# A fifth raw-weight buffer and a softmax denominator summed in one operation

## The chip, the core and the metric

The kernel runs on one core of a Trainium2 chip. The metric is the device time of one execution in microseconds; of several executions the median counts. Inside a core, TensorE (PE) multiplies matrices and has a separate row in the profile for loading weights (PEld); VectorE (DVE), ScalarE (ACT) and GpSimd (POOL) work on tiles; SyncE (SP) issues most of the DMA transfers. Each engine works through its own queue in order, and an instruction that waits holds up all that stands behind it on that engine.

## The reference, cut to what matters

Two layers of a diffusion backbone. 512 latent tokens and 256 context tokens, model width 1024. Each layer has one input projection into three groups of heads (short convolution, windowed attention with a sink, gated linear attention, below called GLA), one output projection, and a SwiGLU block of width 2816. The part that the change touches is the attention's softmax:

```python
def softmax_with_sink(scores, sink):
    s = broadcast(sink, scores.shape[:-1] + (1,))
    p = softmax(concatenate([s, scores], axis=-1), axis=-1)
    return p[..., 1:]

def one_block(qi, i):                       # 128 queries; 8 heads, 2 key heads
    s_ctx = q @ k_ctx                       # 256 context keys
    s_loc = where(valid, q @ ks, -inf)      # up to 3 blocks of 128 keys
    p = softmax_with_sink(concatenate([s_ctx, s_loc]) * HEAD_DIM ** -0.5, sink)
    return p[..., :L] @ v_ctx + p[..., L:] @ vs
```

The sink is one learned number per head that enters the denominator and has no value of its own. Layer 0 also computes attention for the 256 context tokens (over the context keys alone); layer 1 does not.

## The kernel before, in words

Activations stand transposed, features on the 128 partitions, tokens along the free axis. Nearly every float32 product is taken as three products of rounded parts: a value is split into a high part (`whi`, rounded to fp32r) by ScalarE and a low part (`wlo`, the difference) by VectorE, and TensorE runs high times high, high times low, low times high.

**Weights.** A list (`plan`) holds all weight pieces in the order of their use, up to 512 KB each, and among them the pieces of `w_mod`, from which the modulation vectors are made. `w_load` (DMA issue at L523) walks the list and issues the loads on SP's queue. The destinations are the tiles `raw`, a ring of `RAWS = 4` buffers: a load is emitted only once the piece four places earlier has been read, and on the chip it waits until that buffer's readers are done. `w_advance` splits the next piece into `whi` and `wlo` (two buffers each). A `w_mod` piece is not split: either TensorE reads it from `raw` (32-column products with `cst`), or VectorE sums it row by row (`t<-raw,cst,t`, L199).

**Order.** A planner (`Plan`) writes the program out. It keeps an estimated clock for each engine, adds the cost of each operation, and lets short chains of work (`attn_task`, `gla_task`, the pieces of the modulation) in between the large products when their operands should be ready and buffers are free. `ROOM` tells it how many buffers each pool has: `main` and `bank` are banks of PSUM, `act` large tiles, `t3` the temporaries that the profile calls `t`. Until the first products of layer 0 are done (`S.strict`), each engine's order is pinned to the planner's; after that it follows the planner where nothing else decides.

**One attention task** (`attn_task`, 40 of them: 24 in layer 0, of which 8 on context queries, and 16 in layer 1; 32 have local keys) takes one head of each of the two key heads and 128 queries. TensorE makes scores, VectorE takes their maximum (`mx`) and from it `nm`, the negative of the scaled maximum, bounded by the sink. ScalarE takes the exponentials with `nm` as bias and sums each row on the side (`accum_out` into `den` and `den2`; in the profile each such sum is an ACTIVATION_READ_ACCUMULATOR). Then `es` becomes the reciprocal of the denominator: VectorE adds `psink` and `nm`, ScalarE takes the exponential, VectorE adds `den`, adds `den2` where there are local keys, and inverts. TensorE transposes the probabilities, multiplies them with the values, and with `es` broadcast (`bank<-tab,es`) turns the denominators into rows.

**Silu of the gate.** The tiles `gg0` and `gg1` of the input projection go through Silu on ScalarE as they leave TensorE. Silu and Exp are in different tables of ScalarE. `preload` and the Silu itself bring the table loads (ACT_TABLE_LOAD).

The tile `zero` (128 by 512, bfloat16) is the moving operand of 22 products that warm TensorE or open and close shared PSUM banks.

Of the kernel before, what the change touches and what calls it, by code (L numbers as in the profile page):

```python
# [11 lines left out]
BF16 = mybir.dt.bfloat16  # L12
U8 = mybir.dt.uint8
AF = mybir.ActivationFunctionType
ALU = mybir.AluOpType
AX = mybir.AxisListType

P = 128
# [17 lines left out]

LAG = 2600
LAG_F = 2100
ROOM = dict(main=3, bank=5, act=20, t3=14)


XS = (0, SX, 0)
# [48 lines left out]
class Plan:  # L91
# [141 lines left out]
    def free(self, owner=None):  # L233

        now = self.clk["pe"]
        self.live = [e for e in self.live if e[2] is None or e[2] > now]
        left = dict(ROOM)
        used = {g: dict.fromkeys(ROOM, 0) for g in self.kept}
        for e in self.live:
# [80 lines left out]
def hybrid_kernel(ctx: ExitStack, tc: tile.TileContext, x, c, cx, c_ctx, w_mod, b_mod, norm1_g, norm2_g,  # L320
                  w_in, conv_w, attn_sink, gla_gate_w, gla_gate_b, gla_norm_g, w_out, w_up, w_down,
                  final_norm_g, table, out):
    nc = tc.nc
    S = Plan(tc)
    const = ctx.enter_context(tc.tile_pool(name="const", bufs=1))
    wp = ctx.enter_context(tc.tile_pool(name="wp", bufs=2))
    act = ctx.enter_context(tc.tile_pool(name="act", bufs=ROOM["act"]))
    t3 = ctx.enter_context(tc.tile_pool(name="t3", bufs=ROOM["t3"]))
    small = ctx.enter_context(tc.tile_pool(name="small", bufs=4))
    dram = ctx.enter_context(tc.tile_pool(name="dram", bufs=1, space=bass.MemoryType.DRAM))  # L330

    psum = {k: ctx.enter_context(tc.tile_pool(name=k, bufs=ROOM[k], space=bass.MemoryType.PSUM))
            for k in ("main", "bank")}

    def bank(kind="bank"):
        return S.took(kind, psum[kind].tile([P, 512], F32, tag=kind, name=kind))
# [7 lines left out]
    def sm(n, name, bufs=None):  # L344
        return small.tile([P, n], F32, tag=name, name=name, bufs=bufs)


    RAWS = 4
    plan = []

    def cols(src, n):
# [158 lines left out]
    def w_load():  # L510
        while at["dma"] < len(plan):
# [4 lines left out]
            else:  # L516
                if len(ring) >= RAWS and not ring[-RAWS]["read"]:
                    break
                ring.append(it)
                raw = wp.tile([P, 1024], F32, tag="raw", name="raw", bufs=RAWS)  # L520
            it["raw"] = raw[:, :it["n"] * it["width"]].rearrange("p (k n) -> p k n", k=it["n"])
# [107 lines left out]
    psink = const.tile([P, 16], F32, name="psink")  # L629
# [1 line left out]

    ones = const.tile([P, 1], F32, name="ones")
    nc.gpsimd.memset(ones, 1.0)
    zero = const.tile([P, 512], BF16, name="zero")
    nc.gpsimd.memset(zero, 0.0)
    epsc = const.tile([P, 1], F32, name="epsc")
    nc.gpsimd.memset(epsc, EPS)

# [133 lines left out]
    class Opened:  # L772
# [20 lines left out]
        def close(self, evict):  # L793
            for s, pt in zip(self.segs, self.pts):
                self.chunks([len(self.X) - 1], s, pt)
                evict(self.w[0], s, pt)
                S.gave(pt)
            S.poll()

    class Firsts:  # L800
# [5 lines left out]
        def open(self):  # L806
            n = len(self.widths)
            whole = self.pair[0][1] - self.pair[0][0] == 512
            m = ROOM["main"] if whole else 1
            S.room(main=m, bank=n - m + (2 if whole else 0))  # L810
            px = [bank("main" if i < m else "bank") for i in range(n)]
            pc = [bank() for _ in range(n // 2)] if whole else []
            a, b = self.pair
            self.banks = px, pc
            self.at = {a: [(px[i], 0) for i in range(n)],
                       b: [(pc[i // 2], i % 2 * 256) if whole else (px[i], 256) for i in range(n)]}

            self.shared = pc if whole else px
            for pt in self.shared:
                S.mm(pt, zero[:, :P], zero, True, False)  # L820

        def weights(self, q):
            self.parts[q] = w_next((*self.key, q))
# [15 lines left out]

        def close(self):  # L840
            for pt in self.shared:
                S.mm(pt, zero[:, :P], zero, False, True)
            S.poll()

        def run(self, norm, evict, hook=None):
# [635 lines left out]
    def attn_task(l, b, g, st):  # L1481

        loc = [t for t in (b - 1, b, b + 1) if 0 <= t < 4] if b < 4 else []
# [27 lines left out]
        sk = slice(l * 8 + g, l * 8 + g + 5, 4)  # L1511
        nm = sm(2, "nm")
        S.stt(nm, mx, -0.125, nsink[:, sk], ALU.mult, ALU.min)
        den = sm(2, "den")
        den2 = sm(2, "den2")
        st["todo"][g] -= 1
        if st["todo"][g] == 0:
            S.gave(Q)
# [3 lines left out]
        pr = [tmp(), tmp()]  # L1522
        for kv in range(2):
            S.act(pr[kv][:, :256], pc[:, kv * 256:(kv + 1) * 256], AF.Exp, bias=nm[:, kv:kv + 1], scale=0.125,
                  accum_out=den[:, kv:kv + 1])
            if loc:
                S.act(pr[kv][:, 256:nkeys], pl[kv][:, :nl], AF.Exp, bias=nm[:, kv:kv + 1], scale=0.125,
                      accum_out=den2[:, kv:kv + 1])
        S.gave(pc, *pl)
        es = sm(2, "es")  # L1530
        S.tt(es, nm, psink[:, sk], ALU.add)
        S.act(es, es, AF.Exp)
        S.tt(es, es, den, ALU.add)
        if loc:
            S.tt(es, es, den2, ALU.add)
        S.recip(es, es)

        n = len(tiles)
# [2 lines left out]
        pt = [bank() for _ in range(3 if loc else 1)]  # L1541
# [92 lines left out]
    r = rstd(ssum, NT, between)  # L1634
    pt = bank()
    for _ in range(WARM):
        S.mm(pt, zero[:, :P], zero, True, True)
    S.gave(pt)
    pv = bank()
    S.tr(pv[:, :16], vrow[:16, 0, :], ident[:16, :16])  # L1640
# [7 lines left out]
    for t0, t1, _ in (XS, CS):  # L1648
        pt = bank()
# [85 lines left out]
    for l in range(DEPTH):  # L1735
# [104 lines left out]
        def after(name):  # L1840
# [21 lines left out]
            elif name == "v":  # L1862
                tasks["v"] = S.spawn(tokens_task(tmps.pop(name), st["V"]), prio=-1)
            elif name[0] == "q":
                qr = tmps.pop(name)
                rope(qr)
                S.room(act=1)
                Q = act_t(F32R)
                for kv in range(2):
                    own = slice(kv * 64, kv * 64 + 64)  # L1870
                    oth = slice(64 - kv * 64, 128 - kv * 64)
                    S.acopy(Q[own, kv, :n], qr[own, :n])
                    S.tt(Q[oth, kv, :n], qr[own, :n], Q[own, kv, :n].bitcast(F32), ALU.subtract)
                st["q"][i] = Q
                S.gave(qr)
                at_ = max(S.last, st["tk"])

                def when():
                    return max(at_, tasks["v"]["ready"]) if tasks["v"]["done"] else None
                for b in range(nblk):  # L1880
                    tasks["attn"].append(S.spawn(attn_task(l, b, i, st), prio=10 + i, group=("attn", 3), when=when))
# [151 lines left out]
        else:  # L2033
# [3 lines left out]
            def final_task(seg, sums):  # L2037
# [10 lines left out]
                for t in range(nt):  # L2048
                    yield dict(bank=2)
                    pts = [bank(), bank()]  # L2050
                    for k in range(NK):
                        S.tr(pts[k // 4][:, (k % 4) * P:(k % 4 + 1) * P], xT[k][:, t0 + t * P:t0 + (t + 1) * P], ident)
                    o = wp.tile([P, 1024], F32, tag="raw", name="raw", bufs=RAWS)
                    S.ts(o[:, :512], pts[0], r[:, t:t + 1], None, ALU.mult)
# [33 lines left out]
```

## Time and profile before

| | us |
|---|---|
| median of 3 runs | 1610.41 |
| lowest and highest | 1608.43, 1613.43 |
| the profiled execution, its own time | 1607.56 |
| its span, from the first to the last instruction | 1605.8 |
| TensorE busy in it | 1576.7 |
| VectorE busy | 1197.3 |
| ScalarE busy | 763.7 |

The granted clock of TensorE was 0.999 over the span. Busy times of TensorE include the modelled ends of overlapping products, so a gap between two products of less than about 0.17 us doesn't show as idle: a product with 512 columns has a mean duration of some 0.40 us, yet in dense stretches the next one begins 0.23 us after it. Where a row of a timeline says x5, five instructions of one kind are merged; what stands in brackets at its end is idle time ahead of it and what ended it.

### The profile page before, as it was taken

What the parts mean: (1) busy time and instruction counts of PE and PEld (TensorE: products, weight loads), DVE (VectorE), ACT (ScalarE), POOL (GpSimd) and SP (SyncE); (2) the same over time, 40 slices, a digit from 0 to 9 for tenths busy, and PEclk for the clock granted to TensorE, in tenths of its full rate; (3) what the DMA queues carried; (4) which work ended last, traced back from release to release, by engine and by line L of the source; (5) the groups of instructions that cost most, each with busy time, mean ns of one, the idle gap of its engine ahead of it and who ended that gap; (6) DMA issues with size and microseconds to landing.
All of it is one profiled execution on the core that took longest, in us unless ns stands there. A gap on an engine that the chain in (4) does not pass through costs nothing.

```text
span 1605.8 us, 29431 instructions
## 1 busy us (share of the span) xinstructions
PE 1576.7 (98%) x11684; PEld 1392.3 (87%) x11690; DVE 1197.3 (75%) x2386; ACT 763.7 (48%) x1634; POOL 105.2 (7%) x122
## 2 busy tenths in 40 slices
PE   7999999999999999999999999999999999999998
PEld 5777777888889899999999988787879999989898
DVE  5686967658895887788888877869777956757476
ACT  4454635553663243242433546455564744536254
POOL 2000000000000000000000010000001112213012
PEclk9999999999999999999999999999999999999999
DMA  9832221243224544535334342211224466858652
GB/s 267 255 100 55 77 82 37 68 157 107 78 80 131 169 136 122 167 121 153 94 107 129 91 132 66 54 28 54 67 89 116 86 153 144 174 132 159 144 122 92
DMA packets 277578, 184.39 MB, mean 115 GB/s; under 512 B 30853, under 2 KB 258753, under 8 KB 277441
## 3 DMA queue, kind: packets, MB, share of 16 engines
q1 hardware_dynamic: 251008, 155.93, 33.9%
q0 software_dynamic: 24608, 21.27, 7.7%
q10 hardware_dynamic: 1824, 5.31, 0.8%
q8 instruction: 92, 1.51, 0.4%
q14 instruction: 46, 0.37, 0.1%
HBM read 175.14 MB, written 7.34 MB: 114 GB/s over the span
## 4 chain that ended last, share of the span: by engine, by line
PE 82%; DVE 7%; ACT 2%; issue 2%; DMA 1%; DVEq 0%; ACTq 0%
PE main L139 53%; PE bank L139 26%; PE bank L143 3%; DVE act L188 3%; DVE t L188 1%; ACT t L155 1%; DMA raw<-in_w_mod_dram 1%; DVE mx L207 1%; DVE wlo L188 1%; DVE t L216 1%; DVE t L199 0%; DMA raw<-in_w_up_dram 0%; ACT whi L177 0%; ACT act L155 0%; ACT t L177 0%
## 5 line engine op out<-in xcount | busy, mean ns | idle before, releaser
L139 PE MATMUL main<-act,whi 128*128 128x512 f32 (+2 forms) x2772 | 665.4, 345 | 3.5 <-ACT act L155 1.8
L139 PEld LDWEIGHTS main<-act,whi 128*128 128x128 f32 x2772 | 460.0, 189 | 63.1 <-issue 11.6
L139 PE MATMUL main<-act,wlo 128*128 128x512 f32 (+2 forms) x1866 | 478.3, 334 | 1.2 <-DVE wlo L188 1.2
L139 PEld LDWEIGHTS main<-act,wlo 128*128 128x128 f32 x1866 | 314.8, 189 | 27.7 <-DVE wlo L188 2.7
L177 ACT CAST whi<-raw 128x512 fp32r<-128x512 f32 (+4 forms) x242 | 181.4, 751 | 286.3 <-PE main L139 198.9
L139 PE MATMUL bank<-act,whi 128*128 128x256 f32 (+2 forms) x1140 | 208.4, 309 | 0.4 <-DVE whi L188 0.4
L139 PEld LDWEIGHTS bank<-act,whi 128*128 128x128 f32 x1140 | 178.2, 190 | 7.1 <-DVE whi L188 0.8
L139 PE MATMUL bank<-act,wlo 128*128 128x256 f32 (+2 forms) x898 | 170.8, 308 | 0.1
L199 DVE SCALAR_TENSOR_TENSOR act<-main,mods,act 128x256 f32<-128x256 f32 (+1 forms) x162 | 99.0, 615 | 79.0 <-PE main L139 77.8
L188 DVE TENSOR_TENSOR wlo<-raw,whi 128x1024 fp32r<-128x1024 f32 (+4 forms) x122 | 123.1, 1009 | 33.1 <-ACT whi L177 28.9
L139 PEld LDWEIGHTS bank<-act,wlo 128*128 128x128 f32 x898 | 142.6, 190 | 3.9 <-DVE wlo L188 0.6
L177 ACT COPY t<-bank 128x512 f32<-128x512 f32 (+3 forms) x171 | 67.7, 411 | 111.7 <-PE bank L139 96.0
L188 DVE TENSOR_TENSOR wlo<-raw,wlo 128x512 fp32r<-128x512 f32 x120 | 81.7, 686 | 40.4 <-ACT wlo L177 39.8
L199 DVE SCALAR_TENSOR_TENSOR t<-raw,cst,t 128x512 f32<-128x512 f32 x126 | 92.0, 746 | 16.8 <-DMA raw<-in_w_mod_dram 16.1
L188 DVE TENSOR_TENSOR whi<-raw,whi 128x512 fp32r<-128x512 f32 x120 | 81.4, 686 | 27.4 <-ACT whi L177 25.9
L155 ACT ACTIVATE t<-bank,nm 128x256 f32<-128x256 f32 (+1 forms) x144 | 69.9, 498 | 55.8 <-DVE nm L199 52.0
L177 ACT CAST wlo<-raw 128x512 fp32r<-128x512 f32 x120 | 74.6, 622 | 41.3 <-PE main L139 18.9
L188 DVE TENSOR_TENSOR act<-t,act 128x128 fp32r<-128x128 f32 (+7 forms) x150 | 84.3, 575 | 9.5 <-ACT act L177 8.7
L177 ACT CAST act<-t 128x128 fp32r<-128x128 f32 (+6 forms) x142 | 71.6, 521 | 34.0 <-DVE t L188 28.9
L188 DVE TENSOR_TENSOR t<-bank,t 128x256 f32<-128x256 f32 (+4 forms) x129 | 55.4, 431 | 39.9 <-ACT t L177 30.5
L139 PE MATMUL main<-act 128*128 128x256 f32 (+1 forms) x516 | 78.5, 308 | 0.0
L155 ACT ACTIVATE t<-t 128x256 f32<-128x256 f32 (+3 forms) x108 | 58.0, 537 | 40.9 <-DVE t L188 40.3
(161 smaller groups left out, 2012.7 us busy)
## 6 DMA issues: line engine op xcount, KB each, us to landing
raw<-in_w_mod_dram SPq DMA_DIRECT2D x92, 512.0 KB, 4.1
raw<-in_w_up_dram SPq DMA_DIRECT2D x80, 512.0 KB, 4.7
raw<-in_w_in_dram SPq DMA_DIRECT2D x26, 512.0 KB, 3.9
t<-in_w_up_dram POOLq DMA_DIRECT2D x40, 256.0 KB, 5.3
raw<-in_w_down_dram SPq DMA_DIRECT2D x24, 384.0 KB, 4.6
raw<-in_w_down_dram SPq DMA_DIRECT2D x32, 256.0 KB, 2.9
raw<-in_w_down_dram SPq DMA_DIRECT2D x16, 320.0 KB, 3.5
raw<-in_w_up_dram POOLq DMA_DIRECT2D x20, 256.0 KB, 4.7
```

The source lines that it names most:

```text
L139: self.pin("pe", self.nc.tensor.matmul(out, lhsT, rhs, start=start, stop=stop, **kw))
L143: self.pin("pe", self.nc.tensor.transpose(out, in_, ident))
L155: ins = self.pin("act", self.nc.scalar.activation(out, in_, func, **kw))
L177: self.pin("act", self.nc.scalar.copy(out, in_))
L188: self.pin(eng, self._v(eng).tensor_tensor(out, a, b, op))
L199: self.pin(eng, self._v(eng).scalar_tensor_tensor(out, a, s, b, op0, op1))
L207: self.pin("dve", self.nc.vector.tensor_reduce(out, in_, AX.X, op))
L216: self.pin("dve", self.nc.vector.copy_predicated(out, mask, data))
```

## The change

Four edits. `RAWS` becomes 5, and `ROOM["t3"]` becomes 13 in exchange. The tile `zero` shrinks to 128 by 128 (`zeros`), and where 512 columns are needed one of its columns is read with a broadcast. In `attn_task` one tile holds all parts of the denominators in columns: for each of the two heads the sum over context keys, the sum over local keys if there are any, and the exponential of the sink. That exponential is taken by two ScalarE operations of one column each, with `nm` as bias, straight from `psink`; one reduction on VectorE sums the columns.

```diff
-ROOM = dict(main=3, bank=5, act=20, t3=14)
+ROOM = dict(main=3, bank=5, act=20, t3=13)
...
-    RAWS = 4
+    RAWS = 5
...
-    zero = const.tile([P, 512], BF16, name="zero")
-    nc.gpsimd.memset(zero, 0.0)
+    zeros = const.tile([P, P], BF16, name="zeros")
+    nc.gpsimd.memset(zeros, 0.0)
+    zero = zeros[:, :1].to_broadcast([P, 512])
...
-        den = sm(2, "den")
-        den2 = sm(2, "den2")
+
+        nd = 3 if loc else 2
+        den = sm(2 * nd, f"den{nd}")
...
             S.act(pr[kv][:, :256], pc[:, kv * 256:(kv + 1) * 256], AF.Exp, bias=nm[:, kv:kv + 1], scale=0.125,
-                  accum_out=den[:, kv:kv + 1])
+                  accum_out=den[:, kv * nd:kv * nd + 1])
             if loc:
                 S.act(pr[kv][:, 256:nkeys], pl[kv][:, :nl], AF.Exp, bias=nm[:, kv:kv + 1], scale=0.125,
-                      accum_out=den2[:, kv:kv + 1])
+                      accum_out=den[:, kv * nd + 1:kv * nd + 2])
         S.gave(pc, *pl)
         es = sm(2, "es")
-        S.tt(es, nm, psink[:, sk], ALU.add)
-        S.act(es, es, AF.Exp)
-        S.tt(es, es, den, ALU.add)
-        if loc:
-            S.tt(es, es, den2, ALU.add)
+        for kv in range(2):
+            S.act(den[:, (kv + 1) * nd - 1:(kv + 1) * nd], psink[:, l * 8 + g + 4 * kv:l * 8 + g + 4 * kv + 1], AF.Exp,
+                  bias=nm[:, kv:kv + 1])
+        S.red(es, den.rearrange("p (a b) -> p a b", a=2), ALU.add)
         S.recip(es, es)
```

Since the planner's costs, its buffers and the moment of each load change, the order of instructions changes too, in the two attention and GLA stages for the most part. Counted over the program, VectorE loses 112 small additions and gains 40 reductions, ScalarE loses 40 small exponentials and gains 80, and two table loads; TensorE, POOL and SP keep their instructions. On TensorE 818 lines of some 10,000 stand elsewhere, and the number of changes from one kind of product to another is the same before and after.

On VectorE, in the second attention task of layer 0, from its `nm` to its reciprocal (`act<-act` and `t_1085` are GLA work in between; `mx_1542` belongs to the task after it). Before:

```order
L199 SCALAR_TENSOR_TENSOR nm<-mx,nsink 128x2
L216 COPY_PREDICATED t_1085<-lvm,bank 128x384
L188 TENSOR_TENSOR es<-nm,psink 128x2
L188 TENSOR_TENSOR act<-act 128x12x2x32
L207 TENSOR_REDUCE mx<-bank 128x2
L188 TENSOR_TENSOR es<-es,den 128x2
L188 TENSOR_TENSOR act<-act 128x2x12
L207 TENSOR_REDUCE mx_1542<-bank 128x1
L188 TENSOR_TENSOR es<-es,den_1489 128x2
L207 TENSOR_REDUCE mx_1542<-bank 128x1
L220 RECIPROCAL es<-es 128x2
```

And after, at the same place:

```order
L199 SCALAR_TENSOR_TENSOR nm<-mx,nsink 128x2
L216 COPY_PREDICATED t_1087<-lvm,bank 128x384
L188 TENSOR_TENSOR act<-act 128x12x2x32
L207 TENSOR_REDUCE mx<-bank 128x2
L188 TENSOR_TENSOR act<-act 128x2x12
L207 TENSOR_REDUCE mx_1541<-bank 128x1
L207 TENSOR_REDUCE es<-den_1489 128x2
L207 TENSOR_REDUCE mx_1541<-bank 128x1
L220 RECIPROCAL es<-es 128x2
```

Three additions went, and one reduction stands between two maxima of the next task.

On ScalarE, at the Silu of `gg1` in layer 0 (`t_3845` and `t_3876` before, `t_3818` and `t_3890` after, are its latent and its context half; the other rows are attention tasks). Before:

```order
L155 ACTIVATE es<-es 128x2
L155 ACT_TABLE_LOAD
L155 ACTIVATE t_3845<-main 128x512
L155 ACTIVATE t_3876<-main 128x256
L166 ACT_TABLE_LOAD
L177 CAST act<-t_3845 128x512
L177 CAST act<-t_3876 128x256
L155 ACTIVATE t_3905,den<-bank,nm 128x256
```

And after:

```order
L155 ACTIVATE den_3802<-psink,nm 128x1 x2
L155 ACT_TABLE_LOAD
L155 ACTIVATE t_3818<-main 128x512
L166 ACT_TABLE_LOAD
L177 CAST act<-t_3818 128x512
L155 ACTIVATE t_3868,den_3867<-bank,nm 128x256 x2
L155 ACTIVATE t_3869,den_3867<-bank,nm 128x256 x2
L155 ACTIVATE den_3867<-psink,nm 128x1 x2
L177 COPY t_3803<-bank 128x256
L155 ACT_TABLE_LOAD
L155 ACTIVATE t_3890<-main 128x256
L166 ACT_TABLE_LOAD
```

The two halves were under one pair of table loads and are now under a pair each, with an attention task's exponentials between them.

On SP, near the end of the first layer's first products (`t_832` and `csn` are the constants of the masks and of the rotary embedding):

```order
 L523 DMA raw<-in_w_in_dram 128x8x64 x2
-L644 DMA t_832<-in_table_dram 128x768
-L645 DMA csn<-in_table_dram 128x1024
 L523 DMA raw<-in_w_mod_dram 128x4x256
+L645 DMA t_834<-in_table_dram 128x768
+L646 DMA csn<-in_table_dram 128x1024
 L523 DMA raw<-in_w_in_dram 128x8x128
```

One more weight load is issued ahead of the constants. It is the only place where SP's order changes.

## Rows read from the trace of the kernel before

**Rows 1.** The page, part 1: busy time, share of the span, instructions.

```profile
PE 1576.7 (98%) x11684; PEld 1392.3 (87%) x11690; DVE 1197.3 (75%) x2386; ACT 763.7 (48%) x1634; POOL 105.2 (7%) x122
```

**Rows 2.** Windows: busy us of each engine (instructions), then PEclk, DMA share, GB/s.

```profile
20.00:60.00 40.00, 36.59 (x382) 29.22 (x381) 24.14 (x54) 16.16 (x30) 0.00 (x0) 1.00 1.00 251
...
250.00:350.00 100.00, 99.75 (x834) 82.12 (x832) 65.05 (x199) 56.51 (x180) 2.14 (x4) 1.00 0.26 85
...
610.00:720.00 110.00, 109.24 (x652) 101.55 (x651) 84.32 (x143) 36.27 (x65) 0.00 (x0) 1.00 0.45 136
```

**Rows 3.** Waits of PEld, 102 to 440 us: us in total, times, longest.

```profile
PEld bank L139 <- ACT t L177: 3.7, 6, 1.1
...
PEld bank L143 <- DVE t L203: 0.8, 2, 0.7
...
PEld bank L139 <- ACT es L155: 0.4, 1, 0.4
...
PEld bank L139 <- DVE es L188: 0.2, 1, 0.2
```

**Rows 4.** The same, 1000 to 1310 us.

```profile
PEld bank L139 <- ACT t L177: 4.5, 8, 1.4
...
PEld bank L139 <- DVE act L188: 1.2, 3, 0.7
...
PEld bank L139 <- DVE t L188: 0.2, 1, 0.2
PEld bank L143 <- ACT act L177: 0.2, 1, 0.2
```

**Rows 5.** Groups by shape: busy us, mean ns of one, idle before and releasers.

```profile
L155 ACT ACTIVATE t<-bank,nm 128x256 f32<-128x256 f32 x112 | 52.2, 475 | 55.8 <-DVE nm L199 52.0 <-PE main L139 1.6 <-DVE es L220 1.3
...
L155 ACT ACTIVATE t<-bank,nm 128x384 f32<-128x384 f32 x32 | 18.6, 581 | 0.0
...
L188 DVE TENSOR_TENSOR es<-es,den 128x2 f32<-128x2 f32 x72 | 11.2, 155 | 16.1 <-ACT es L155 15.4
...
L207 DVE TENSOR_REDUCE mods<-bank 128x4 f32<-128x16 f32 x8 | 1.4, 172 | 9.3 <-PE bank L143 9.3
```

**Rows 6.** Timeline of ACT around the Silu of gg1, layer 0: start, us.

```profile
328.04 0.47 ACT L155 ACTIVATE t<-bank,nm 128x256 f32<-128x256 f32 x1 [2.51 <-DVE nm L199]
328.41 0.19 ACT L155 ACTIVATION_READ_ACCUMULATOR t<-bank,nm 128x1 f32 x1
...
330.07 0.21 ACT L155 ACTIVATE es<-es 128x2 f32<-128x2 f32 x1
330.16 0.49 ACT L155 ACTIVATE t<-bank,nm 128x256 f32<-128x256 f32 x1
...
331.30 1.28 ACT L155 ACT_TABLE_LOAD   x1
332.60 0.87 ACT L155 ACTIVATE t<-main 128x512 f32<-128x512 f32 x2
```

**Rows 7.** Waits of VectorE, whole span.

```profile
DVE t L199 <- DMA raw<-in_w_mod_dram: 16.1, 16, 4.0
```

**Rows 8.** Timelines of ACT, then PE, 34 to 37 us.

```profile
34.27 1.00 ACT L177 CAST whi<-raw 128x960 fp32r<-128x960 f32 x1 [0.67 <-DMA raw<-in_w_in_dram]
...
36.51 0.50 PE L139 MATMUL main<-act,wlo 128*128 128x512 f32 x1 [0.69 <-DVE wlo L188]
```

**Rows 9.** Timelines of DVE, then PE, 637 to 641 us.

```profile
637.91 0.75 DVE L199 SCALAR_TENSOR_TENSOR t<-raw,cst,t 128x512 f32<-128x512 f32 x1 [4.03 <-DMA raw<-in_w_mod_dram]
...
640.50 0.50 PE L139 MATMUL main<-act,wlo 128*128 128x512 f32 x1 [0.17 <-DVE wlo L188]
```

**Rows 10.** The tile csn: its readers, and its DMA.

```profile
L188 DVE TENSOR_TENSOR t<-t,csn x20: 674/689/702, 77.4 to 1098.9; 128x512 f32<-128x512 f32 x20
L645 SPq DMA_DIRECT2D csn<-in_table_dram x1: 434/434/434, 64.2 to 64.2; - x1
...
DMA to landing us min/median/max: 4.4/4.4/4.4
```

More of the change, by code (lines that the diff above doesn't have):

```diff
@@ L819, in open @@
             for pt in self.shared:
-                S.mm(pt, zero[:, :P], zero, True, False)
+                S.mm(pt, zeros, zero, True, False)
         def weights(self, q):
@@ L841, in close @@
             for pt in self.shared:
-                S.mm(pt, zero[:, :P], zero, False, True)
+                S.mm(pt, zeros, zero, False, True)
             S.poll()
@@ L1636, in hybrid_kernel @@
     for _ in range(WARM):
-        S.mm(pt, zero[:, :P], zero, True, True)
+        S.mm(pt, zeros, zero, True, True)
     S.gave(pt)
```

## The prediction

> **What bounds the kernel now.** I read the page's busy times first, then the windows by stage, then what TensorE's weight loads wait for, and last the timelines of the places where a wait shows. TensorE is busy for 1576.7 of 1605.8 us [rows 1]. What it doesn't fill is 29.1 us, and that is the most that any edit which leaves its products alone can return, apart from gaps too short to show. It is less in the stages: between 250 and 350 us, where attention tasks run among the projections, TensorE is busy 99.75 of 100 us, VectorE 65.05 and ScalarE 56.51 [rows 2]. The two slower engines there have time to spare in sum and matter only by their latency: a product waits when the tile that it needs comes out of a queue a little late.
>
> So the question for every edit is not how much busy time it takes off VectorE or puts on ScalarE, but how much of that reaches a waiting product. The waits of the weight loads tell which engine is the late one. From 102 to 440 us they wait for ScalarE in 7 rows, from 3.7 us down to 0.4 us, 8.3 us together, and for VectorE in 8 rows, from 0.8 down to 0.2 us, 3.6 us together [rows 3]. From 1000 to 1310 us it is 9 rows for ScalarE, from 4.5 down to 0.2 us, together 11.4 us, and 7 for VectorE, from 1.2 down to 0.2 us, together 4.0 us [rows 4]. ScalarE is late by 19.7 us, VectorE by 7.6 us. These are upper bounds, since a weight load can wait while the product before it still runs. The denominators themselves hardly appear: products wait for `es` in rows of 0.4 and 0.2 us [rows 3].
>
> **The sum.** I make it against the profiled execution, 1607.56 us, which is 1.76 us more than its span and 2.85 us under the median of the three runs.
>
> *The denominators on VectorE.* An addition on two columns takes 155 ns [rows 5]. The change takes out 72 additions of `den` and 40 of `psink`, 112 by 0.155, 17.4 us, and puts in 40 reductions. A reduction of 16 columns to 4 takes 172 ns [rows 5]; for 4 or 6 columns I take the same, 6.9 us. VectorE's busy time falls by 10.5 us. How much of it reaches a product lies between nothing and the 7.6 us that weight loads wait for VectorE. The two stages are some 550 us long, and at the share of the window at 250 us [rows 2] VectorE works some 360 us in them; 10.5 us are 3% of that, and 3% of 7.6 us is 0.2 us. I take -0.2. The wait in these chains does not go: VectorE stood 15.4 us, in front of the first addition, until the exponential of `es` was there [rows 5]. Now the reduction stands there and waits for ScalarE's last column.
>
> *The denominators on ScalarE.* One exponential of two columns goes, two of one column with `nm` as bias come, 40 times. The old one occupied the engine for 0.09 us, from 330.07 to the next start at 330.16 [rows 6]. For the new one the nearest row is the exponential with the same bias on 256 columns: it starts at 328.04 and the engine goes on at 328.41 [rows 6], 0.37 us. The step from 256 to 384 columns, 475 to 581 ns [rows 5], gives 0.83 ns a column, so 256 columns are 0.21 us and what remains for one column is 0.16 us. Bounds for one: 0.09 us, as the old one without a bias tile, and 0.37 us. At 0.16 a task gains 2 by 0.16 less 0.09, 0.23 us, and all 40 gain 9.2 us; at the bounds 3.6 and 26 us. Queued behind these 0.23 us on ScalarE are the copies of the transposed probabilities, evictions and the next weight's high part. The engine has idle time in every one of these stages, 43 of 100 us in the window at 250 us [rows 2], and gives most of it back there. By the same share it works some 310 us in the two stages; 9.2 us are 3% of that, and 3% of the 19.7 us is 0.6 us. I take +0.6, and keep 0 and 9.2 as ends; 26 us would need the old neighbour's 256 columns in an operation that has one, so I don't carry that end.
>
> The Trainium skill (ScalarE: Activation LUTs, What ACT_TABLE_LOAD costs) states 186 ns plus 0.833 ns a column for an activation, 93 ns more when the bias is a column of a tile, and an overlap of 93 ns between neighbours. The slope agrees with the trace; by the page a new exponential occupies 0.19 us instead of my 0.16, and the 40 tasks would add some 11 us by that estimate. No row shows one on a single column.
>
> *The chain of one task.* The last column is there later by 0.23 us less the little that the additions took: one addition of 155 ns fewer follows in the tasks with local keys, none in the 8 others. The denominators come 0.1 to 0.2 us later. Ahead of their use lie the transposes, their copies and a stretch of large products, and the waits for `es` were 0.4 and 0.2 us [rows 3]. Nothing on the path; if that cover were gone it would be at most 40 by 0.2, 8 us.
>
> *The second pair of table loads at `gg1`.* The Silu of the context half now has loads of its own. One load takes 1.28 us and the Silu begins 1.30 us after its start [rows 6], so ScalarE gets 2.6 us more at that place. What waits behind them are the copies of an attention task and the high part of the next weight, and after them the output projection, whose first pass is over the latent tokens and doesn't need the context half. ScalarE is idle nearly half of the time there. I take 0, between 0 and 2.6. The Trainium skill (same page, same section) counts 1.28 us for the load and 1.38 us more to drain, 2.66 us for each switch, and asks to group activations by table. By it the pair costs 5.3 us; the row shows that the engine goes on 0.02 us after the load, so I stay with 2.6.
>
> *The fifth raw buffer.* A load can now be issued one piece earlier. It helps where a product waits for something that waited for a load. Two such places show: at 34.27 us ScalarE waits 0.67 us for a load and 2 us later TensorE stands for 0.69 us [rows 8]; at 637.91 us VectorE has waited 4.03 us for a piece of `w_mod`, behind which stand an eviction and the low part of a weight, and at 640.50 us TensorE stands for 0.17 us [rows 9]. VectorE's waits for such loads come to 16.1 us in 16 places [rows 7]. Those are the two ends: nothing, and -16.1 us if each were on the path and went. Between 20 and 60 us the DMA engines are full, share 1.00 [rows 2]; an earlier issue lands no earlier there, it only joins the line. Between 610 and 720 us the share is 0.45 [rows 2], and an earlier issue does land earlier. Of the 16.1 us only a few tenths reach TensorE in the one place that I can follow, so I take an eighth, -2.0.
>
> *The constants behind one more load.* On SP the tables are issued behind a load that waits for its buffer. `csn` was issued at 64.2 us, landed 4.4 us later, and is first read at 77.4 us [rows 10]: over 8 us of slack. Nothing.
>
> *`zeros` and one `t3` tile fewer.* The products with `zeros` have the same shape and number; the broadcast read is not in the trace. I take 0: the 22 products have their old number of columns, and a slower read would show on them alone. One temporary fewer shows only through the order.
>
> *The order.* TensorE has the same products and as many switches from kind to kind, so no stage gets denser by design. Which waits fall where is drawn anew in the two stages: 27.3 us of waits [rows 3, 4], of which I let a fifth go either way, 5.5 us. I take 0.
>
> Sum: -0.2 +0.6 +0 +0 -2.0 +0 +0 +0 = -1.6 us, 1606.0 us for an execution like the profiled one, and 1610.41 - 1.6 = 1608.8 us on the median. That is 0.1% less. About 0.3%, 4.8 us, is what a measurement of this kernel can tell from no change, so I forecast no change.
>
> **The rivals.** *ScalarE becomes the late engine (slower).* The 0.23 us of every task falls ahead of the copies on which products wait most, 3.7 and 4.5 us in the first rows [rows 3, 4]. If all of it passes, with the pair of table loads, it is 9.2 + 2.6 = 11.8 us, 1622 us on the median; half of it, some 6 us, gives 1616. It decides from about 4.8 us on, when over 40% passes. For it: ScalarE is the later engine of the two by more than two to one. Against it: the idle time beside it.
>
> *The fifth buffer takes most of the late loads (faster).* If the places of [rows 7] held back evictions and through them the products by half, it is -8 us, 1602. For it: in-order VectorE stands up to 4 us at a time with evictions behind it. Against it: TensorE stood 0.17 us after the longest one [rows 9], because several banks were open.
>
> *The order alone.* The stages shift by 5.5 us one way or the other, 1605 or 1616. For it: 818 places on TensorE differ. Against it: the planner works by the same rules, and the kinds of waits stay.
>
> *The fifth buffer does nothing.* The splits into `whi` and `wlo` still have two buffers each, and these set the pace; then -2.0 falls away and 1610.8 us is left.
>
> **How the numbers follow.** The forecast gets 0.40; ScalarE late 0.17 (0.13 of it over 0.3%); late loads 0.18 (0.15 over 0.3%); the order 0.15 (0.07 each way); the buffer without effect 0.10. Faster by over 0.3%: 0.15 + 0.07 = 0.22. Slower: 0.13 + 0.07 = 0.20. Within: 0.58. The range reaches from the late loads at -8 us, with a little of the order's gain, to ScalarE late by half: 1600 to 1617 us.
>
> **What would show it.** In the profile of the changed kernel: VectorE's busy time lower by about 10 us and ScalarE's higher by 9 to 14 us; a small exponential that occupies ScalarE for 0.16 us; VectorE's wait in front of the reduction still near 15 us; two more table loads around the Silu of `gg1`; VectorE's waits for `w_mod` well under 16.1 us; and TensorE's idle time within 5 us of 29. I would be wrong if the weight loads' waits for ScalarE grew by over 5 us in the two stages, or if the waits for loads fell and the span fell by as much.

## The result and the profile after

The changed kernel is slower: 1619.09 us on the median of 6 runs (1617.89 to 1623.18) against 1610.34 us of the kernel before (1608.43 to 1613.43), a ratio of 1.0049 with the interval 1.0029 to 1.0069. I had forecast 1608.8 us and a range up to 1617: the sign is wrong and the time lies above the range. The profiled execution took 1617.89 us with a span of 1616.1. The one of the kernel before, 1607.56 us, is faster than each of its six runs, so the two profiles lie 10.3 us apart where the medians lie 8.8 apart.

The page's busy times, then the windows of the stretches of [rows 2] and of a short one at the first place below (length, busy us of PE, PEld, DVE, ACT, POOL with their instructions, granted clock, DMA share, GB/s):

```profile
PE 1582.0 (98%) x11684; PEld 1399.3 (87%) x11690; DVE 1194.8 (74%) x2314; ACT 775.8 (48%) x1676; POOL 104.3 (6%) x122
```

```profile
20.00:60.00 40.00, 37.31 (x378) 29.95 (x379) 23.92 (x53) 15.49 (x30) 0.00 (x0) 0.96 1.00 257
250.00:350.00 100.00, 97.95 (x795) 80.75 (x796) 60.18 (x166) 59.69 (x183) 2.14 (x4) 0.98 0.25 85
610.00:720.00 110.00, 109.32 (x656) 102.53 (x655) 87.09 (x144) 38.55 (x67) 0.00 (x0) 1.00 0.45 133
262.90:266.30 3.40, 3.40 (x18) 3.01 (x16) 2.58 (x11) 2.87 (x10) 0.00 (x0) 0.50 0.49 154
```

Against [rows 1] VectorE is busy for 2.5 us less and ScalarE for 12.1 us more. But TensorE is busy for 5.3 us more with the same 11,684 products, and its idle time grows from 29.1 to 34.1 us. The fourth window shows where the busy time comes from: for 3.4 us after 262.9 us the granted clock is 0.50, that is 1.2 instead of 2.4 GHz, and each product takes longer. Over the whole span the mean granted clock is 0.995, against 0.999 before. Not all of that is the change's: the 0.96 of the first window stands in g2_all_oldorder below too. In the attention window at 250 us TensorE does 795 products instead of 834 [rows 2].

I counted how late each product starts against the kernel before, the same product in both. The profiled execution ends 10.6 us later, and three places make up most of it: 3.2 us around 262 us, 2.8 us around 530 us, some 4 us between 1105 and 1130 us. What lies between and behind them nearly cancels; in the attention stages the figure swings by several us where products have changed places.

**The first place, layer 0's attention.** ScalarE, then TensorE, of the changed kernel (start, duration, operation, idle time and its releaser):

```profile
260.32 1.04 ACT L177 CAST whi<-raw 128x1024 fp32r<-128x1024 f32 x1 [3.50 <-PE main L139]
261.27 0.47 ACT L155 ACTIVATE t<-bank,nm 128x256 f32<-128x256 f32 x1
...
263.29 0.48 ACT L155 ACTIVATE den<-psink,nm 128x1 f32<-128x1 f32 x2
263.66 0.58 ACT L177 COPY t<-bank 128x512 f32<-128x512 f32 x1
```

```profile
260.12 0.28 PE L139 MATMUL main<-act,wlo 128*128 128x256 f32 x1
262.44 0.50 PE L139 MATMUL bank<-act 128*128 128x256 f32 x2 [2.05 <-ACT t L155]
```

The cast of the next weight stands ahead of the task's exponentials. It waits 3.50 us for TensorE to finish with its buffer; only behind it can the exponentials read the score banks, and TensorE stands 2.05 us for such a bank; 0.45 us after it goes on, its clock falls. Before, the exponentials came first, the cast behind them, and TensorE stood 0.20 us:

```profile
257.91 0.48 ACT L155 ACTIVATE t<-bank,nm 128x256 f32<-128x256 f32 x1 [2.84 <-DVE nm L199]
...
260.50 1.07 ACT L177 CAST whi<-raw 128x1024 fp32r<-128x1024 f32 x1
```

```profile
259.09 0.50 PE L139 MATMUL bank<-act 128*128 128x256 f32 x2 [0.20 <-ACT t L155]
```

**The second place, layer 0's down projection.** VectorE, then TensorE, of the changed kernel:

```profile
524.16 1.54 DVE L199 SCALAR_TENSOR_TENSOR t<-raw,cst,t 128x512 f32<-128x512 f32 x2 [2.42 <-DMA raw<-in_w_mod_dram]
527.55 1.54 DVE L199 SCALAR_TENSOR_TENSOR t<-raw,cst,t 128x512 f32<-128x512 f32 x2 [1.84 <-DMA raw<-in_w_mod_dram]
529.00 0.74 DVE L199 SCALAR_TENSOR_TENSOR act<-main,mods,act 128x512 f32<-128x512 f32 x1
```

```profile
529.89 0.70 PE L139 MATMUL main<-act,whi 128*128 128x512 f32 x2 [2.53 <-DVE act L199]
```

Four sums of `w_mod` with waits for loads of 2.42 and 1.84 us stand ahead of the residual's eviction, and TensorE waits 2.53 us for it. Before, the evictions came first, the sums behind them, and TensorE had no gap there:

```profile
521.50 1.14 DVE L199 SCALAR_TENSOR_TENSOR act<-main,mods,act 128x512 f32<-128x512 f32 x2 [2.35 <-PE main L139]
...
525.08 1.53 DVE L199 SCALAR_TENSOR_TENSOR t<-raw,cst,t 128x512 f32<-128x512 f32 x2
```

The wait that the fifth buffer was to take away is still there, 15.9 us for 16.1 [rows 7]:

```profile
DVE t L199 <- DMA raw<-in_w_mod_dram: 15.9, 14, 2.4
```

**The third place, layer 1's attention.** TensorE stands four times within 6 us, and its clock is at half for 6.8 us:

```profile
1112.02 1.09 PE L139 MATMUL bank<-act 128*128 128x256 f32 x6 [1.53 <-DVE mx L188]
...
1113.63 0.62 PE L139 MATMUL bank<-act 128*128 128x384 f32 x2 [0.40 <-ACT t L155]
...
1115.74 0.76 PE L139 MATMUL bank<-act,t 64*64 64x64 f32 x32 [1.36 <-ACT t L177]
1117.94 0.79 PE L139 MATMUL main<-act,wlo 128*128 128x512 f32 x1 [1.45 <-DVE wlo L188]
```

```profile
1116.20:1123.00 6.80, 5.36 (x33) 4.48 (x26) 6.15 (x14) 4.38 (x15) 0.00 (x0) 0.50 0.49 144
```

Which instruction was moved to make these waits I didn't trace, and no run below changes this place alone.

### The profile page after: what moved, and what is told of

It reads as the page before. It is cut to its first block, busy times and chain, and to the rows that moved or that the text cites. A ratio compares the mean times of both kernels' runs of the same rounds, so it can differ in the third digit from the quotient of the medians.

```text
span 1616.1 us, 29398 instructions
## 1 busy us (share of the span) xinstructions
PE 1582.0 (98%) x11684; PEld 1399.3 (87%) x11690; DVE 1194.8 (74%) x2314; ACT 775.8 (48%) x1676; POOL 104.3 (6%) x122
## 4 chain that ended last, share of the span: by engine, by line
PE 86%; DVE 7%; DMA 3%; ACT 2%; issue 2%; DVEq 0%; SPq 0%; ACTq 0%
PE main L139 55%; PE bank L139 28%; PE bank L143 3%; DVE act L188 2%; DVE wlo L188 1%; DVE t L188 1%; DMA act<-in_w_mod_dram 1%; DMA raw<-in_w_mod_dram 1%; ACT t L155 1%; ACT whi L177 1%; DVE t L199 0%; DVE mx L207 0%; DVE t L216 0%; DMA act<-in_x_dram 0%; ACT act L155 0%
## 5 line engine op out<-in xcount | busy, mean ns | idle before, releaser
L199 DVE SCALAR_TENSOR_TENSOR t<-raw,cst,t 128x512 f32<-128x512 f32 x126 | 91.8, 746 | 16.5 <-DMA raw<-in_w_mod_dram 15.9
L177 ACT COPY t<-main 128x256 f32<-128x256 f32 (+2 forms) x112 | 49.8, 448 | 55.4 <-PE main L139 54.8
```

Source lines behind the costliest of these rows:

```text
L177: self.pin("act", self.nc.scalar.copy(out, in_))
L199: self.pin(eng, self._v(eng).scalar_tensor_tensor(out, a, s, b, op0, op1))
```

## The experiments

My first theory (A) was that the fifth buffer's order did it, since both gaps look like a planner that believes loads to be early. The rivals were the work of the new exponentials (B) and that any order drawn anew shifts the time (C). Each ratio is against the kernel before on the same chip, where it took 1611.7 us (the first four), 1611.4 (the next four), 1613.6 (then three) and 1612.5 (the last four).

### One part at a time

**e1_softmax**, only the new softmax on the kernel before (the hunks of the diff above that lie in `attn_task`):

> The kernel before with the softmax edit alone: the denominators in columns of one tile, one reduction, the sink's exponential with a bias per head. Four raw buffers, 14 t3 tiles, the old zero tile. Theory A (the slowdown of 8.7 us comes from the order that the fifth raw buffer draws: the w_mod sums ahead of the residual evictions near 530 us, the cast of the next weight ahead of an attention task's exponentials near 262 us): this kernel stays within 4 us of the kernel before, some 1610 us, TensorE's gap near 530 us is absent and the granted clock falls only in the tail. Theory B (the two added exponentials of every task, 40 times some 0.3 us of ScalarE, pass to TensorE): some 1618 to 1620 us, and the weight loads' waits for ScalarE from 102 to 440 and from 1000 to 1310 us grow from 19.7 us by about 8. Theory C (any new order shifts the time by several us whatever the edit): a time off 1610 by 3 to 9 us, either way, with gaps in other places than those of the changed kernel.

Measured: 1622.62 us, 1.0065 (1.0035 to 1.0096).

**e2_raw5**, all of the change but the softmax (`RAWS = 5`, `t3=13`, `zeros`):

> The changed kernel with the old softmax: five raw buffers, 13 t3 tiles and the broadcast zeros on the kernel before. Theory A: 1616 to 1620 us, with the gap of about 2.5 us near 530 us, where two w_mod sums stand ahead of the residual on VectorE. Theory B: 1608 to 1611 us. Theory C: off 1610 by 3 to 9 us, with gaps elsewhere.

Measured: 1613.82 us, 1.0009 (0.9993 to 1.0025).

**e3_small**, only `t3=13` and `zeros`:

> The kernel before with 13 t3 tiles and the broadcast zeros alone: four raw buffers, the old softmax. Theories A and B: as the kernel before, 1608 to 1612 us. Theory C: the order is drawn anew in a part of the program (a third as many lines of difference as with the other edits), so a shift of up to 5 us. If the broadcast read is slow, the 22 products with zeros are longer than in the kernel before, and nothing else is.

Measured: 1615.45 us, 1.0019 (0.9997 to 1.0042).

**e4_noraw5**, the changed kernel with `RAWS = 4`:

> The changed kernel with four raw buffers instead of five, all else as in it: the new softmax, 13 t3 tiles, the broadcast zeros. Theory A: 1608 to 1612 us, no gap near 530 us. Theory B: 1618 to 1620 us, as the changed kernel. Theory C: anything within 9 us of 1610, with gaps in places that neither of the two kernels has.

Measured: 1621.34 us, 1.0054 (1.0031 to 1.0077).

Theory A falls for the loss: the fifth buffer alone is not slower, and without it the loss is all there. It was right for one place: near 530 us TensorE stands 1.77 us in e2_raw5 and not at all in e1_softmax and e4_noraw5. The gap of 2.05 us near 262 us is in all three kernels with the new softmax. So the loss goes with the softmax edit, by its work or by the order that it draws; part by part this can't be told, since the scheduler reorders on every edit.

### The same order, instruction by instruction

So I held the order. The new kernel creates its instructions in the same sequence as the kernel before (the planner is charged the old operations), and each engine's queue is then chained in the order in which the kernel before runs it (shortened; `given` unpacks a stored list):

```diff
+    def replay(self):
+        for engine, log in self.log.items():
+            place = {int(k): i for i, k in enumerate(given(engine))}
+            log = sorted(log, key=lambda e: (place[int(np.floor(e[0]))], e[0]))
+            for a, b in zip(log, log[1:]):
+                self.behind(b[1], a[1])
```

**f1_newops_oldorder**, new softmax instructions in the old order:

> The kernel before with the new softmax instructions, and every engine's queue held in the order of the kernel before, instruction by instruction: the second exponential of a task stands right behind the first, the reduction where the first addition of the exponential stood. Theory W (the work of the new instructions is the cost: 40 times some 0.28 us more on ScalarE ahead of the copies, as the softmax edit alone lost 10.9 us on the median): 1617 to 1623 us. Theory O (the cost is the order that the scheduler drew for them): 1609 to 1614 us, no gap of 2 us near 260 us and no fall of the granted clock there.

Measured: 1614.89 us, 1.0024 (1.0011 to 1.0038). It lies between the two ranges, 0.9 us above that of theory O; the gap near 260 us is 0.20 us and the clock stays, as theory O had it.

**f2_oldops_neworder**, old softmax instructions in the order of e1_softmax:

> The old softmax instructions of the kernel before, in the order that the kernel with the softmax edit alone has on every engine: one exponential of es in the place of the two, the two additions in the place of the reduction. Theory W: back at 1609 to 1614 us. Theory O: 1617 to 1625 us like the kernel whose order it has, with the cast of a weight ahead of a task's exponentials near 262 us, TensorE's gap of 2 us there and the clock at half behind it.

Measured: 1620.22 us, 1.0054 (1.0037 to 1.007). This decides it: with not one new instruction, 8.8 us are lost, of the 10.9 us of e1_softmax. The old instructions have the gap near 262 us too:

```profile
264.55 0.50 PE L206 MATMUL bank<-act 128*128 128x256 f32 x2 [2.05 <-ACT t L231]
```

```profile
264.55:267.95 3.40, 3.23 (x20) 2.33 (x21) 3.13 (x16) 2.60 (x9) 0.00 (x0) 1.00 0.54 153
```

One thing that I expected is missing: behind this gap the clock stayed at 1.00. The loss doesn't need it.

**g2_all_oldorder**, the whole change in the old order (the planner still counts four buffers, the pool has five):

> The whole change, new softmax instructions, five raw buffers, 13 t3 tiles and the broadcast zeros, in the order of the kernel before on every engine (the loads are issued in the old order too; a load only finds its buffer free one piece earlier). Theory W: 1616 to 1623 us. Theory O: 1608 to 1613 us; by the terms of my prediction without the order, 1.6 us less than the kernel before on the same chip.

Measured: 1608.91 us, 0.9982 (0.9973 to 0.9991). In the old order the change makes the kernel faster by 2.5 us. Its own order takes 10.2 us, from 1608.91 to 1619.09 by the medians, and 10.8 by the two ratios, which compare each with the kernel before beside it.

**g1_raw5_oldorder**, the same without the softmax:

> Five raw buffers, 13 t3 tiles and the broadcast zeros with the old softmax, in the order of the kernel before on every engine. Both theories: within 2 us of the kernel before. If an earlier load is worth what my prediction gave it, 2 us less; VectorE's waits for the loads of w_mod, 16.1 us in the kernel before, fall to under 8. If one t3 tile fewer makes a chain wait, slower by up to 3 us with new waits for buffers.

Measured: 1605.79 us, 0.9962 (0.9949 to 0.9975), and the runs lie within 1.4 us (1605.26 to 1606.70), while the 23 of the kernel before beside them reach from 1607.38 to 1615.79. By the fastest of each the gain is 2.1 us, by the medians 5.6, more than the 2 us that I expected. VectorE's wait of [rows 7] in this kernel (its lines are numbered higher by the code that holds the order):

```profile
DVE t L273 <- DMA raw<-in_w_mod_dram: 0.3, 1, 0.3
```

and the place of [rows 9]: the sum that waited 4.03 us waits 0.30, and the eviction now waits for TensorE, as it should.

```profile
635.70 0.75 DVE L273 SCALAR_TENSOR_TENSOR t<-raw,cst,t 128x512 f32<-128x512 f32 x1 [0.30 <-DMA raw<-in_w_mod_dram]
639.18 1.14 DVE L273 SCALAR_TENSOR_TENSOR act<-main,mods,act 128x512 f32<-128x512 f32 x2 [2.74 <-PE main L204]
```

In g2_all_oldorder the first place reads, on ScalarE and TensorE:

```profile
260.86 0.48 ACT L1612 ACTIVATE den<-psink,nm 128x1 f32<-128x1 f32 x2
261.23 0.59 ACT L251 COPY t<-bank 128x512 f32<-128x512 f32 x1
261.69 1.07 ACT L251 CAST whi<-raw 128x1024 fp32r<-128x1024 f32 x1
```

```profile
260.01 0.50 PE L204 MATMUL bank<-act 128*128 128x256 f32 x2 [0.20 <-ACT t L229]
```

The exponentials come first, the cast behind a copy, and TensorE stands 0.20 us.

Two more comparisons lie in these runs. e2_raw5 and g1_raw5_oldorder have the same buffers and, but for one pair of table loads that g1 has more, the same instructions in two orders: 1.0009 and 0.9962, 7.6 us apart. So the order that these edits drew costs about as much as the softmax's; in e2_raw5 it is hidden behind what the buffer gives. And no run chains the kernel before in its own order, so the comparisons with it hold the chaining as well. The chained kernels among themselves say that it matters little: from f1 to g2 the fifth buffer with `t3` and `zeros` gives 6.0 us, from the kernel before to g1 5.6.

### What the new softmax instructions cost

In the old order they cost 3.5 us on four buffers (f1 against the kernel before) and 3.1 us on five (g2 against g1), by the medians. **h1_one_exp** goes back to one exponential for both heads and keeps the columns and the reduction:

```diff
+        S.tt(es, nm, psink[:, sk], ALU.add)
+        S.act(den[:, nd - 1::nd], es, AF.Exp)
```

> As the run with the whole change in the order of the kernel before, but the sink's exponential again one operation of two columns, on the sum that VectorE makes as before; it writes into the two columns of the denominators' tile, and the one reduction stays. Five raw buffers, 13 t3 tiles, broadcast zeros, the order of the kernel before. Theory X (the second exponential and the bias on ScalarE make the 3.1 us by which the new softmax instructions lose in the old order): 1605 to 1607 us on the scale on which the kernel before has 1611.4, that is 5 us under it. Theory R (the reduction with its later denominators makes them): 1608 to 1610 us.

Measured: 1605.49 us, 0.9952 (0.9934 to 0.997). That is 8.1 us under the kernel before beside it, more than the 5 us of theory X, and can't be told from g1's 0.9962; against g2's 0.9982 the intervals don't overlap. So the cost goes with the pair of biased exponentials in place of one addition and one exponential, and for the reduction nothing is left that these runs could tell. The exponentials and the reduction, by shape, in g2_all_oldorder and then in h1_one_exp (busy us, mean ns, idle before):

```profile
L1618 DVE TENSOR_REDUCE es<-den 128x2 f32<-128x6 f32 x32 | 5.0, 155 | 20.0 <-ACT den L1612 19.8
...
L1612 ACT ACTIVATE den<-psink,nm 128x1 f32<-128x1 f32 x80 | 19.4, 300 | 0.0
```

```profile
L229 ACT ACTIVATE den<-es 128x2 f32<-128x2 f32 x40 | 8.5, 213 | 0.0
```

### Moving single instructions back

If two places cost 3.2 and 2.8 us in the changed kernel, moving what stands wrong there should return it. Here the changed kernel's own order is held in the same way, but for the places of a few instructions (the code below is a sketch; the kernels hold the finished lists). **h2_cast_moved** puts the one cast of 260.32 us behind the task's exponentials; **h3_cast_and_sums_moved** also puts the four sums of 524 to 528 us behind the evictions:

```diff
+act_order = move(act_order, [cast_whi], behind=last_den_exponential)
+dve_order = move(dve_order, four_mod_sums, behind=second_wlo)
```

> The changed kernel, every queue in its own order but for one instruction: on ScalarE the cast of a weight near 260 us stands behind the six exponentials of the attention task instead of ahead of them. If that one place costs what the trace shows, TensorE's gap of 2.05 us at 262.4 us goes, with it the granted clock at half for 3.41 us, and the time falls by 3 us against the changed kernel, to some 1616 us. If the waits only move to the next tile, the time stays at 1619.

> As the run with the cast moved, and on VectorE the four w_mod sums near 524 to 528 us stand behind the residual evictions and the low parts of two weights instead of ahead of them. If the place costs what the trace shows, TensorE's gap of 2.53 us at 529.9 us goes and the time falls by another 2.8 us, to some 1613 us. If the sums' loads hold the raw buffers and delay what follows, the gap comes back later and the time stays.

Measured: 1620.30 us, 1.0042 (1.0025 to 1.0058), and 1619.84 us, 1.0039 (1.0024 to 1.0053). Neither can be told from the changed kernel's 1.0049. TensorE around the first place in h2_cast_moved:

```profile
261.40 0.51 PE L211 MATMUL bank<-act 128*128 128x256 f32 x2 [0.43 <-ACT t L236]
264.20 1.14 PE L215 MATMUL bank<-tab,t 128*128 128x128 f32 x8 [1.13 <-ACT t L258]
267.22 0.79 PE L211 MATMUL main<-act,whi 128*128 128x512 f32 x1 [1.87 <-DVE t L269]
```

The gap of 2.05 us became 0.43, and 1.13 and 1.87 us appeared behind it: the copies that now stand behind the cast are late, and then VectorE, which reads a `main` bank out late. The clock fell there again. The second gap, which this run leaves alone, was 3.10 us in its profile. In h3_cast_and_sums_moved it did go. On VectorE, and on TensorE at two places:

```profile
528.83 0.75 DVE L279 SCALAR_TENSOR_TENSOR act<-main,mods,act 128x512 f32<-128x512 f32 x1 [4.25 <-PE main L210]
...
532.80 3.10 DVE L279 SCALAR_TENSOR_TENSOR t<-raw,cst,t 128x512 f32<-128x512 f32 x4
```

```profile
530.04 0.63 PE L210 MATMUL main<-act,whi 128*128 128x512 f32 x2
...
648.66 0.95 PE L210 MATMUL main<-act,whi 128*128 128x256 f32 x3 [0.87 <-DVE act L279]
```

The sums no longer wait at all, and TensorE goes on without a gap at 530 us. In the profiled execution 2 us of that were lost again at 650 us, where a gap of 0.87 us was followed by 3.4 us at half clock. So a gap names what was late in this order; it is not the amount that one move returns. That the order costs is shown; which places of it make up the 10 us is not.

### Orders that nothing asked for

Is any order drawn anew worse? Four kernels change only a number of the planner, for example:

```diff
-    HOP = 150
+    HOP = 145
```

> The kernel before, all its instructions and buffers, with one number of the planner changed: the step that it counts from one engine to the next, 145 instead of 150. Nothing is different but the order: 292 rows of TensorE's queue in another place. Theory L (the order of the kernel before is a low point, and any order drawn anew costs): 3 to 10 us slower than the kernel before on the same chip. Theory S (it is the softmax edit and the fifth buffer that draw bad orders): within 3 us of the kernel before, either way.

> The kernel before with the planner's fixed cost of a VectorE operation at 66 instead of 62. Only the order differs, 269 rows of TensorE's queue. Theory L: 3 to 10 us slower. Theory S: within 3 us.

> The kernel before with the planner's rate of a load at 0.33 instead of 0.31 MB per us. Only the order differs, and little: 67 rows of TensorE's queue. Theory L: 1 to 5 us slower, less than the two others. Theory S: within 3 us.

> The kernel before with the planner's step from engine to engine at 165 instead of 150. Only the order differs, 347 rows of TensorE's queue, the most of the four. Theory L: 3 to 10 us slower. Theory S: within 3 us.

Measured: n2 1618.95 us, 1.0031 (1.0011 to 1.0052); n3 1617.05 us, 1.0018 (0.9996 to 1.0041); n4 1612.20 us, 0.9992 (0.997 to 1.0013); n5 1615.22 us, 1.0012 (0.9993 to 1.0031). By the ratios that is -1 to +5 us, against 8.7 and 10.8 us for the orders of the softmax edit and of the whole change. One is slower beyond doubt, two lean that way with intervals that reach down to no change, and the one that moves least stays where it was. Neither theory is borne out: L is too large for n4 and n5, S too small for n2. The new orders also change the table loads: 15 in n2, 11 in n3 and n5, 13 in n4 and in the kernel before, so a pair more may be part of n2's loss. Why the edits' orders are worse than these is open.

## Why the prediction was wrong

- **The order, "I take 0"**: this is the step that failed. It gave 5.5 us either way from the waits of weight loads. Measured: +10.2 us for the whole change, +8.8 for the softmax edit. The size was wrong because I took it from the wrong place: the weight loads' waits in the two attention stages, 27.3 us, of which I let a fifth move. In the changed kernel they are 31.3 us, only 4.0 more. The place at 530 us lies outside both stages; and a new order makes gaps of TensorE of 1.5 to 2.5 us, where the longest of the kernel before after its first 30 us was 1.17. Behind some of them the clock falls: e1_softmax has a mean clock of 0.9946 over its runs, the kernel before beside it 0.9975, which is at most some 5 of its 10.9 us (an estimate: the missing share of the clock times the time); f2 has 0.9963 for 0.9977, some 2 of its 8.8 us. With the same products on TensorE, what is left are its waits. The middle was wrong because I took up and down as equally likely: of four orders that nothing asked for, none gained beyond the scatter of the runs.
- **The argument against that rival**, "the planner works by the same rules, and the kinds of waits stay": the rules stayed, but their input didn't. With five buffers the planner counts loads as earlier and puts the sums ahead of the evictions, as the rows at 524 to 529 us show. The cast at 260 us comes with the softmax's new costs instead, in e1_softmax with four buffers.
- **The fifth buffer, -2.0**: right in direction, too small in the old order (-5.6 by the medians, -2.1 by the fastest runs, -6.0 from f1 to g2). The waits for `w_mod` went from 16.1 to 0.3 us there; in the changed kernel they are back at 15.9. Of the alternatives, "late loads" was right for the buffer by itself, and "does nothing" was right for its waits in the order that the change drew.
- **ScalarE, +0.6**: mis-sized. One new exponential occupies 0.185 us, by the pair at 263.29 us and the next start at 263.66; I had 0.16. A task gains 0.28 us, all 40 gain 11.2. The estimate by the figures of the Trainium skill (ScalarE: Activation LUTs, What ACT_TABLE_LOAD costs) was 0.19, and the trace agrees with it. Of the 11.2 us 3.1 reach the end, 28% and not the 6% that I let pass: spreading the 9.2 us evenly over ScalarE's work was wrong, since they stand where products wait for it. In the old order the weight loads' waits for ScalarE of [rows 3, 4] grow by 2.3 us from g1 to g2, 19.3 to 21.6. (The two stretches of these rows are 648 us long, not the 550 that I spread over; with 648 the term would have been 0.5.) My sign for being wrong, these waits growing by over 5 us, did not show in the changed kernel either, 19.7 to 21.6: it watched ScalarE, and the loss was elsewhere.
- **VectorE, -0.2**: h1, which has the cheaper VectorE work without the new exponentials, has the ratio 0.9952 for g1's 0.9962, no more than the runs can tell. A reduction takes 153 to 157 ns, not 172. Its wait for the exponentials, which I put near 15 us, is 12.2 us in the changed kernel and 24 us in g2 (19.8 of it in the row above, the rest in the tasks without local keys). VectorE's busy time fell by 2.5 us and not by the 10 that I gave as a sign, though the additions' 17.4 us went and only 6.1 us of reductions came; busy time counts overlapping instructions once.
- **Table loads, 0**: 15 loads instead of 13, as forecast. The kernels in the old order have 13, so the pair's price is part of the 10.2 us and was not measured by itself. The loss doesn't need it: e1_softmax and f2 have 13 too.
- **`zeros`, `t3`, `csn`, 0**: in the old order g1 carries the first two and is the second fastest; none shows a cost. e3_small's 1.0019 (its interval reaches 1) has an order of its own.

## What to carry to other kernels

Where a scheduler draws the order, an edit is two changes, its work and its order, and the second can be two to four times the first (8.8 us against 3.5 for the softmax, 10.2 against 2.5 for the whole): hold the old order to measure the work, and put the old work into the new order to measure the order. With TensorE busy 98% of the time a redrawn order has little left to gain; the seven redrawn orders compared here cost -1 to +11 us. So the forecast for such an edit should lean to slower unless the order is kept. Keep the order that is good and give it the edit, as g1 and h1 do: 5.6 and 8.1 us faster than the kernel before beside them.

## What was not expected of the hardware

The clock of TensorE. Two kernels in the old order, g2_all_oldorder and g1_raw5_oldorder, at the same place of layer 1; TensorE's rows, then the windows behind them:

```profile
1113.94 0.69 PE L204 MATMUL bank<-act,t 64*64 64x64 f32 x32 [1.20 <-ACT t L251]
1115.08 0.73 PE L204 MATMUL main<-act,whi 128*128 128x512 f32 x2 [0.45 <-ACT t L251]
```

```profile
1115.90:1119.30 3.40, 3.40 (x56) 3.07 (x54) 1.72 (x5) 1.25 (x4) 0.00 (x0) 0.50 0.00 0
```

```profile
1112.86 0.69 PE L204 MATMUL bank<-act,t 64*64 64x64 f32 x32 [0.93 <-ACT t L251]
1114.00 0.73 PE L204 MATMUL main<-act,whi 128*128 128x512 f32 x2 [0.45 <-ACT t L251]
```

```profile
1114.50:1117.90 3.40, 3.40 (x69) 3.00 (x67) 2.91 (x8) 2.09 (x5) 0.00 (x0) 1.00 0.10 31
```

Behind a wait 0.27 us longer the clock fell to 1.2 GHz for 3.4 us, and 1.6 of the 2.2 us between the two profiled executions arise right there. The longer wait alone doesn't settle it: in f1_newops_oldorder the same rows show 1.20 and 0.45 us, and the clock stayed; and the gap of 2.05 us had the clock fall behind it in the changed kernel and not in f2. So behind the same wait there can be 1.6 us more, or nothing. Part of the scatter from run to run goes with this. Of the 23 runs of the kernel before beside g1, the three slowest (1615.15 to 1615.79 us) have a mean clock of 0.996, the two fastest (1607.38 and 1608.85) 0.999 and 1.000.
